# Stick-breaking attention: ordinary transfers issued by GpSimd, transposing ones by SyncE, and four split tiles instead of three

## The chip, the cores and the metric

The kernel runs on one core of a Trainium2 chip. The core has a matrix engine (TensorE, PE; its weight loads are shown as PEld), VectorE (DVE), ScalarE (ACT), GpSimd (POOL) and SyncE (SP), which computes nothing and only issues transfers. Each engine works through its own queue of instructions in order; semaphores join them. 16 DMA engines move the data. The metric is the device time of one execution in microseconds; lower is better.

## The reference

A decoder of two layers over 1024 positions of width 1024, in float32: a recurrent block (RG-LRU), a dense SwiGLU block, then stick-breaking attention with 16 heads of 64, and a second SwiGLU block, with RMS norms before each. The change touches the attention alone:

```python
def stick_breaking_attention(x, w_qkv, w_o):
    qkv = jnp.einsum("bsd,de->bse", x, w_qkv).reshape(bsz, seq, 3, N_HEADS, HEAD_DIM)
    ...
    for blk in range(seq // Q_BLOCK):
        ...
        z = jnp.einsum("bhqd,bhkd->bhqk", qb, kb).astype(jnp.float32) * scale
        ...
        log_fail = jnp.where(strict, jax.nn.log_sigmoid(-z), 0.0)
        suffix = lax.cumsum(log_fail, axis=3, reverse=True) - log_fail
        weights = jnp.where(strict, jnp.exp(jax.nn.log_sigmoid(z) + suffix), 0.0)
        outs.append(jnp.einsum("bhqk,bhkd->bhqd", weights.astype(vb.dtype), vb))
    ...
    return jnp.einsum("bse,ed->bsd", o, w_o)
```

## The kernel before

Matrix products in float32 are made from split operands: a tile is written as a high part and a rest (`hi`, `lo`), and three products are summed (`mm3`). In the attention the operands are half-precision pairs or float32 pairs, made in the same way.

The attention works on pairs of heads, `q` = 0 to 7. For each pair, `qkv_steps` projects queries, keys and values (`which` = 0, 1, 2) in two halves of 512 positions. It is a generator that yields after every `mm3`, so that its matrix products can be set between those of the pair before: it is the "fill". What it yields is handled by `evacuate`:

- Queries and keys are split into `two` and copied by ordinary transfers into the tiles `q` (four transfers per half, 128 KB each) and `kk` (four per half, 256 KB each), because the parts have to change partitions.
- Values are split into `vx` and brought into `v` by two transposing transfers per half.
- The weight columns for the projections come by `load_raw`, 512 KB each, three per pair, into the tiles `raw`; `load_link` asks for the one after the next.

The scores of one chunk of 128 queries by up to 512 keys are made by `z_part` on PE; `z_rest` (ACT, a sigmoid) and `scan` (DVE, a running product) turn them into the tile `w`; `turn_weights` splits that into the half-precision tile `wx`, first part by ACT (L1676), rest by DVE (L1677), and one transposing transfer (L1681) brings `wx` into `wt`. `av_part` (PE, L1699) multiplies `wt` by `v`. There are 24 chunks and 24 such products ("units") per pair; the chunks run 8 units ahead.

When a row of units is done, `gather` collects the output in `oo`, `add_v` adds the values (L1715, on GpSimd, or on VectorE for the last pair), and `parts` scales and splits it (ACT L1722, DVE L1723). Most of these outputs are parked in device memory (`od`), two transfers each, since their tiles `xh`, `xl` still hold the input of the projections; `bring_back` reloads them when the projections of the last pair are done, 12 transfers for the first half and 14 after the second. `xh`, `xl` are named `vh`, `vl` or `xg` in the trace.

These small jobs wait in the list `later`, of which one is done per unit. The order of all instructions is written out by hand: each engine executes in the order in which the program lists them (`manual_schedule`). SyncE issues every transfer of the attention, the ordinary and the transposing ones, in one queue. Each pool's `bufs` says how many copies of a tile there are: three of `wx`, two of `vx`. The program is built with 1024 bytes of storage for transfers that GpSimd issues (`dynamic_dma_scratch_size=1024`); before the change it issues none.

Of the kernel before, what the change touches and what calls it, by code (L numbers as in the profile page):

```python
# [11 lines left out]
F16 = mybir.dt.float16  # L12
# [5 lines left out]
P = 128  # L18
S = 1024
D = 1024  # L20
ND = D // P
# [13 lines left out]
def trunk(  # L35
# [21 lines left out]
    nc = tc.nc  # L57
    f32 = lambda t: t.bitcast(F32)
# [42 lines left out]
    xh, xl = [None] * ND, [None] * ND  # L101
# [8 lines left out]
    cp.tile([P, 136], F32, name="edge_l")  # L110


    def load_raw(src, shape):
        raw = rp.tile([P, D], F32, tag="raw", name="raw")
        view = raw if len(shape) == 1 else raw.rearrange("p (a b) -> p a b", a=shape[0])
        nc.sync.dma_start(view, src)
        return raw

    def split(raw, pool=None, tag="w", bufs=None, lo_eng=None, parts=1):
# [9 lines left out]
    def cols(w, c0, n=P):  # L129
        return w[:, c0 : c0 + n].rearrange("(k p) c -> p k c", p=P)  # L130
# [24 lines left out]
    class Mix:  # L155
# [5 lines left out]
            for i in range(ahead):  # L161
                self.proc(i)

        def load(self, i):
            self.raw[i] = load_raw(cols(self.src, self.order[i] * P), (ND,))

        def proc(self, i):
            raw = self.raw.pop(i)
# [91 lines left out]
    with ExitStack() as st, tc.manual_schedule(engines={E.PE, E.Activation, E.DVE, E.Pool, E.SP}):  # L260
# [20 lines left out]
        for i in range(2):  # L281
            src = w_in[i * NB : (i + 1) * NB, D : D + P].rearrange("(k p) c -> p k c", p=P)
# [112 lines left out]
    with ExitStack() as st:  # L395
# [17 lines left out]
        two = lp.tile([P, ND], I32, name="two")  # L413
# [136 lines left out]
        with tc.manual_schedule(engines={E.PE}):  # L550
            for what in "A0 A1 B0 A2 G0 A3 Y0 B1 Y1 A4 G1 A5 B2 Y2 A6 G2 A7 B3 Y3 B4 Y4 G3 B5 Y5 B6 Y6".split():
                {"A": stage_a, "B": stage_b, "G": stage_g, "Y": stage_y}[what[0]](int(what[1]))
            mix = last_tile(ND - 1)
# [833 lines left out]
    def finish(h, w, R, pp, rows):  # L1387
# [75 lines left out]
    w_qkv, wq0 = attn_w_qkv[0], []  # L1463
# [10 lines left out]
    od = {  # L1474
        (q, n): [dp.tile([P, NB], F32, name=f"od{x}{q}_{n}") for x in "hl"]
        for n in range(NH)
        for q in range(NP)
        if kept(q, n)
    }

    pos, obs, begun = ExitStack(), ExitStack(), {}
    with ExitStack() as st:
        ap = st.enter_context(tc.tile_pool(name="ap", bufs=1))
        qs, mix = ExitStack(), [Mix(w_o, 0)]
# [13 lines left out]
        Q, KK, VV, VT = {}, {}, {}, {}  # L1498
# [5 lines left out]
        later, raws, sv, av_ = [], {}, {}, {}  # L1504

        def bring_back(*which):
            for q, n in which:
                nc.sync.dma_start(f32(xh[q][n]), od[q, n][0])
                nc.sync.dma_start(f32(xl[q][n]), od[q, n][1])


        def load_link(i):
            q, which = divmod(i, 3)
            if q < NP:
                raws[i] = load_raw(cols(w_qkv, which * D + q * P), (ND,))
            else:
                mix[0].load(which)

        def column_norms(raw, q):
            sq = ap.tile([P, ND, P], BF16, tag="sq", name="sq", bufs=1)  # L1520
# [62 lines left out]
        def evacuate(q, which, n, ps):  # L1583
            full = lambda tag, m: [ap.tile([P, m, S], F32R, tag=tag, name=tag, bufs=4 if m == 1 else 3) for _ in range(2)]
            cs = slice(n * NB, (n + 1) * NB)
            if which == 2:
                if n == 0:
                    VT[q] = ap.tile([P, S + 1], F32, tag="vt", name="vt", bufs=2)
                    nc.gpsimd.memset(VT[q][:, 0:1], 0.0)
                    VV[q] = ap.tile([P, 2, NT, 2, HD], F16, tag="v", name="v", bufs=2)  # L1590
                t = ap.tile([P, NB], F32, tag="t", name="t", bufs=2)
                after = VT[q][:, n * NB + 1 : (n + 1) * NB + 1]
                nc.vector.scalar_tensor_tensor(after, ps, f32(sv[q]), rbc[n], op0=ALU.mult, op1=ALU.mult)
                yield
                nc.vector.tensor_sub(t, VT[q][:, cs], after)
                vx = ap.tile([P, 4, 2, P], F16, tag="vx", name="vx", bufs=2)
                t3 = t.rearrange("p (b c) -> p b c", b=4)
                nc.scalar.activation(vx[:, :, 0], t3, AF.Copy, scale=1 / UP)
                nc.vector.scalar_tensor_tensor(vx[:, :, 1], t3, 1 / UP, vx[:, :, 0], op0=ALU.mult, op1=ALU.subtract)
                for hx, a in enumerate((top, bot)):  # L1600
                    nc.sync.dma_start(
                        VV[q][:, hx, 4 * n : 4 * n + 4].rearrange("p b h c -> p (b h) c"),
                        vx[a].rearrange("p b h c -> p (b h c)"),
                        transpose=True,
                    )
                if q == NP - 1 and n == 0:
                    bring_back(*((p, 0) for p in range(NP - 2)))
                return
            two = ap.tile([P, 2, NB], F32R, tag="two", name="two", bufs=2)
            if which == 0:  # L1610
                t = ps
                if n == 0:
                    Q[q] = [x[:, 0] for x in full("q", 1)]
            else:
                t = ap.tile([P, NB], F32, tag="t", name="t", bufs=2)
                nc.vector.tensor_mul(t, ps, rbc[n])
                if n == 0:
                    KK[q] = full("kk", 2)
            nc.scalar.copy(two[:, 0], t)
            if which == 0:  # L1620
                nc.vector.tensor_sub(two[:, 1], t, f32(two)[:, 0])
            yield
            if which == 1:
                nc.vector.tensor_sub(two[:, 1], t, f32(two)[:, 0])
            for hx, (a, b) in enumerate(((top, bot), (bot, top))):
                if which == 0:
                    nc.sync.dma_start(f32(Q[q][hx])[a, cs], f32(two)[a, 0])
                    nc.sync.dma_start(f32(Q[q][hx])[b, cs], f32(two)[a, 1])
                else:
                    for half_ in (top, bot):  # L1630
                        nc.sync.dma_start(f32(KK[q][hx])[half_, :, cs], f32(two)[a])


        W = {}
# [37 lines left out]
        def turn_weights(q, hx, j, ci, c0, c1, diag):  # L1672
            F = W[q, hx, j, ci].rearrange("p (b c) -> p b c", c=P)
            m = F.shape[1]
            wx = ap.tile([P, 4, 2, P], F16, tag="wx", name="wx", bufs=3)
            nc.scalar.copy(wx[:, 0:m, 0], F)  # L1676
            nc.vector.tensor_sub(wx[:, 0:m, 1], F, wx[:, 0:m, 0])  # L1677
            g = (q, hx, j // 4, ci)
            if g not in T:
                T[g] = ap.tile([P, 8, 4, P], F16, tag="wt", name="wt", bufs=3)  # L1680
            nc.sync.dma_start(  # L1681
                T[g][:, 0 : 2 * m, j % 4], wx[:, 0:m].rearrange("p b h c -> p (b h c)"), transpose=True
            )
# [7 lines left out]
        def av_part(q, hx, G, kb, first, last):  # L1691
            q0 = max(kb - 4 * G, 0)
            if first:
                av[0] = psO.tile([P, NB], F32, tag="o", name="av_ps")
            ps = av[0]
            lhsT = VV[q][:, hx, kb]
            for part in range(2):
                rhs = T[q, hx, G, kb // 4][:, 2 * (kb % 4) + part, q0:]
                nc.tensor.matmul(  # L1699
                    ps[:, q0 * P :], lhsT=lhsT, rhs=rhs, start=first and part == 0, stop=last and part == 1  # L1700
                )
            if not last:
                return
            a, b = (top, bot)[:: 1 if hx == 0 else -1]

            def gather():
                if hx == 0:
                    oo[q, G] = ap.tile([P, NB], F32, tag="oo", name="oo", bufs=2)
                o = oo[q, G]
                nc.scalar.copy(o[a], ps[b])  # L1710
                nc.vector.tensor_add(o[a], ps[a], o[a])

            def add_v():
                eng = nc.vector if q == NP - 1 else nc.gpsimd
                eng.tensor_add(oo[q, G], oo[q, G], VT[q][:, G * NB + 1 : (G + 1) * NB + 1])  # L1715

            def parts():
                o = oo[q, G]
                down = f32(av_[q])

                def both(hi, lo):
                    nc.scalar.activation(hi, o, AF.Copy, scale=down)  # L1722
                    nc.vector.scalar_tensor_tensor(lo, o, down, f32(hi), op0=ALU.mult, op1=ALU.subtract)  # L1723

                if not kept(q, G):
                    both(xh[q][G], xl[q][G])
                else:
                    oh = ap.tile([P, NB], F32R, tag="oh", name="oh", bufs=1)
                    both(oh, o.bitcast(F32R))
                    nc.sync.dma_start(od[q, G][0], f32(oh))  # L1730
                    nc.sync.dma_start(od[q, G][1], o)

            later.insert(0, gather)
            if hx == 1:
                later.extend((add_v, parts))
# [33 lines left out]
        def score(some):  # L1769
            ps = [z_part(*a) for a in some]  # L1770
            while turning:
                turn_weights(*turning.pop(0))
            for a in some:
                z_rest(ps.pop(0), *a)
                scan(*a)
                turning.append(a)

        E = mybir.EngineType
        with tc.manual_schedule(engines={E.PE, E.Activation, E.DVE, E.Pool, E.SP}):


            load_link(1)
            first = qkv_steps(0)
            between = {
# [18 lines left out]
            c = 0  # L1803
# [69 lines left out]
```

## Time and profile before

| | |
|---|---|
| three timed runs, us | 2298.23, 2293.41, 2296.41; median 2296.41 |
| profiled execution, us | 2296.88, with a span of 2295.1 |
| busy in the span | PE 94%, DVE 78%, ACT 50%, POOL 5% |
| DMA queues | SP's 476032 packets, 334.39 MB, 51.7% of 16 engines |
| chain that ended last | PE 73%, DVE 11%, DMA 6% (all of it `wt<-wx`), ACT 6% |
| attention | from about 960 to 1575 us |

A row of the timeline gives the start in us, the duration in us, engine, line, operation, what is written and read, and in brackets the idle time of the engine before it and what ended it. "SPq" is SyncE's queue: its rows are the issuing of transfers, not their duration. A row of the waits gives who waited for whom, the total in us, how often, and the longest. A row of the stretches gives the length, then busy time and count of PE, PEld, DVE, ACT and POOL, the granted clock of PE, the DMA engines' busy share and GB/s. A row of a tile's instructions gives the shortest, median and longest in ns; one of the DMA issues ends with the median time from issue to landing in us.

### The profile page before, as it was taken

Reading aid. Unit: us, or ns where it says so; the run is one execution under the profiler, and the core shown is the slowest. Engines: PE = TensorE matmul, PEld = TensorE weight load, DVE = VectorE, ACT = ScalarE, POOL = GpSimd, SP = SyncE. Lnnn points to the kernel's source line nnn. Section 1 sums busy time; section 2 is a strip of 40 time slices with the busy share of each in tenths; the row PEclk is TensorE's granted clock in tenths of the full one; section 3 lists DMA queues with packets and bytes.
Section 4 is the critical chain, followed back from the end, with each engine's and each line's share of the span. In section 5 each row is a group of like instructions: output and inputs, shape, how many; then the busy total and the mean of one; then the engine's idle time right before and its main releaser. Section 6 shows DMA issues by size and latency. Waiting matters only on the chain.

```text
span 2295.1 us, 27839 instructions
## 1 busy us (share of the span) xinstructions
PE 2148.8 (94%) x9838; PEld 1742.7 (76%) x9838; DVE 1795.2 (78%) x2604; ACT 1136.8 (50%) x1838; POOL 121.2 (5%) x102
## 2 busy tenths in 40 slices
PE   8999999999999999987778878749999999999999
PEld 7888888888888888865556556527888888888887
DVE  7888588888887888867677776746788888878886
ACT  6676445444445455645445444434454444444556
POOL 1222010000000000000000000001100000000002
PEclk9999999999999999999898989869999999999999
DMA  6111422344447745477777776786223444477452
GB/s 221 55 38 56 156 74 92 115 134 156 138 155 267 244 139 159 129 148 156 141 168 149 158 151 146 155 206 194 74 87 111 137 153 141 152 255 263 147 154 90
DMA packets 476331, 336.43 MB, mean 147 GB/s; under 512 B 187288, under 2 KB 383008, under 8 KB 476192
## 3 DMA queue, kind: packets, MB, share of 16 engines
q1 hardware_dynamic: 476032, 334.39, 51.7%
q8 instruction: 77, 1.26, 0.2%
q14 instruction: 62, 0.51, 0.1%
q10 hardware_dynamic: 160, 0.27, 0.0%
HBM read 184.09 MB, written 83.36 MB: 117 GB/s over the span
## 4 chain that ended last, share of the span: by engine, by line
PE 73%; DVE 11%; DMA 6%; ACT 6%; issue 3%; SPq 1%; DVEq 0%; ACTq 0%
PE p_ps L143 16%; PE p_ps L145 16%; PE p_ps L144 16%; DMA wt<-wx 6%; DVE w L1665 3%; PE a_ps L144 2%; PE a_ps L145 2%; DVE w L1668 2%; PE a_ps L143 2%; PE ob_ps L143 2%; PE ob_ps L144 2%; PE ob_ps L145 2%; ACT wx L1676 2%; ACT w L1658 2%; DVE wx L1677 2%
## 5 line engine op out<-in xcount | busy, mean ns | idle before, releaser
L1677 DVE TENSOR_TENSOR wx<-w,wx 128x128 f16<-128x128 f32 (+1 forms) x192 | 107.2, 559 | 138.4 <-ACT wx L1676 135.5
L1676 ACT CAST wx<-w 128x128 f16<-128x128 f32 (+1 forms) x192 | 98.0, 510 | 227.5 <-DMA wt<-wx 113.3
L143 PE MATMUL p_ps<-vh,wbh 128*128 128x512 f32 x524 | 204.8, 391 | 0.0
L144 PE MATMUL p_ps<-vl,wbh 128*128 128x512 f32 x524 | 204.5, 390 | 0.0
L145 PE MATMUL p_ps<-vh,wbl 128*128 128x512 f32 x524 | 204.2, 390 | 0.2 <-DVE wbl L722 0.2
L143 PE MATMUL p_ps<-vh,wch 128*128 128x512 f32 x524 | 204.2, 390 | 0.0
L145 PE MATMUL p_ps<-vh,wcl 128*128 128x512 f32 x524 | 204.0, 389 | 0.0
L144 PE MATMUL p_ps<-vl,wch 128*128 128x512 f32 x524 | 203.9, 389 | 0.0
L718 ACT CAST wbh<-sb 128x1024 fp32r<-128x1024 f32 (+2 forms) x69 | 69.6, 1009 | 191.6 <-DVE sb L702 191.6
L1699 PE MATMUL av_ps<-wt,v 128*128 128x512 f16 (+3 forms) x384 | 107.3, 366 | 60.1 <-DMA wt<-wx 51.3
L145 PE MATMUL p_ps<-vh,wal 128*128 128x512 f32 x396 | 154.3, 390 | 0.1
L143 PE MATMUL p_ps<-vh,wah 128*128 128x512 f32 x396 | 154.1, 389 | 0.0
L144 PE MATMUL p_ps<-vl,wah 128*128 128x512 f32 x396 | 154.1, 389 | 0.0
L143 PE MATMUL qk_ps<-vh,whi 128*128 128x512 f32 x264 | 140.3, 532 | 0.0
L1658 ACT ACTIVATE w<-z_ps,rs 128x128 f32<-128x128 f32 (+1 forms) x192 | 110.7, 577 | 21.8 <-PE z_ps L1646 21.4
L1645 PE MATMUL z_ps<-kk,q 128*128 128x256 f32 (+1 forms) x192 | 75.8, 395 | 47.3 <-ACT w L1658 44.7
L1665 DVE TENSOR_TENSOR_SCAN w<-w,unit 128x128 f32<-128x128 f32 (+3 forms) x128 | 112.4, 879 | 6.6 <-ACT w L1658 2.9
L145 PEld LDWEIGHTS p_ps<-vh,wbl 128*128 128x128 f32 x524 | 98.4, 188 | 22.3 <-DVE wbl L722 1.5
L145 PEld LDWEIGHTS p_ps<-vh,wcl 128*128 128x128 f32 x524 | 98.4, 188 | 21.1 <-DVE wcl L732 0.6
L143 PEld LDWEIGHTS p_ps<-vh,wch 128*128 128x128 f32 x524 | 98.4, 188 | 20.5 <-ACT tb L1177 0.2
L144 PEld LDWEIGHTS p_ps<-vl,wch 128*128 128x128 f32 x524 | 98.4, 188 | 20.3
L143 PEld LDWEIGHTS p_ps<-vh,wbh 128*128 128x128 f32 x524 | 98.6, 188 | 19.2 <-ACT ta L1177 0.2
(396 smaller groups left out, 5781.2 us busy)
## 6 DMA issues: line engine op xcount, KB each, us to landing
raw<-in_ffn_w_in SPq DMA_DIRECT2D x88, 512.0 KB, 4.0
vl<-pd SPq DMA_DIRECT2D x128, 256.0 KB, 3.6
pd<-U SPq DMA_DIRECT2D x90, 256.0 KB, 2.3
kk<-two SPq DMA_DIRECT2D x64, 256.0 KB, 4.2
raw<-in_ffn_w_out SPq DMA_DIRECT2D x56, 256.0 KB, 3.6
raw<-in_attn_w_qkv SPq DMA_DIRECT2D x24, 512.0 KB, 4.9
h<-hd SPq DMA_DIRECT2D x32, 256.0 KB, 5.5
hd<-h SPq DMA_DIRECT2D x32, 256.0 KB, 2.0
```

Of the source, the lines that this page charges most:

```text
L143: nc.tensor.matmul(ps, lhsT=wh, rhs=mh, start=first, stop=False, **kw)
L144: nc.tensor.matmul(ps, lhsT=wh, rhs=ml, start=False, stop=False, **kw)
L145: nc.tensor.matmul(ps, lhsT=wl, rhs=mh, start=False, stop=last, **kw)
L718: nc.scalar.copy(self.full(self.wb), self.full(self.sb))
L1645: nc.tensor.matmul(ps[:, 0 : c1 - c0], lhsT=lhsT, rhs=KK[q][hx][:, 0, c0:c1], start=True, stop=False)
L1658: nc.scalar.activation(F, ps[:, 0:n], AF.Sigmoid, scale=rs[:, j : j + 1])
L1665: nc.vector.tensor_tensor_scan(rev, rev, unit[:, NB - n :][:, ::-1], 0.0, op0=ALU.mult, op1=ALU.add)
L1668: nc.vector.tensor_tensor_scan(rev, rev, rev, first, op0=ALU.mult, op1=ALU.bypass)
L1676: nc.scalar.copy(wx[:, 0:m, 0], F)
L1677: nc.vector.tensor_sub(wx[:, 0:m, 1], F, wx[:, 0:m, 0])
L1699: nc.tensor.matmul(ps[:, q0 * P :], lhsT=lhsT, rhs=rhs, start=first and part == 0, stop=last and part == 1)
```

## The change

Ordinary transfers of the attention go from SyncE's queue to GpSimd's: the copies into `q` and `kk`, the parking of outputs and their reloading, and the weight loads that `load_link` asks for. A weight load on GpSimd is issued as two halves of four blocks each. SyncE keeps the transposing transfers of `wx` and `vx`. `wx` has four tiles instead of three; `vx` has one instead of two. No arithmetic and no matrix product is changed, and the other engines' order stays.

```diff
-    def load_raw(src, shape):
+    def load_raw(src, shape, queue=nc.sync):
         raw = rp.tile([P, D], F32, tag="raw", name="raw")
         view = raw if len(shape) == 1 else raw.rearrange("p (a b) -> p a b", a=shape[0])
-        nc.sync.dma_start(view, src)
+        if queue is nc.sync:
+            queue.dma_start(view, src)
+        else:
+            for i in range(2):
+                c = slice(i * D // 2, (i + 1) * D // 2)
+                queue.dma_start(raw[:, c].rearrange("p (k c) -> p k c", c=P), src[:, 4 * i : 4 * i + 4])
         return raw
...
-        def load(self, i):
-            self.raw[i] = load_raw(cols(self.src, self.order[i] * P), (ND,))
+        def load(self, i, **kw):
+            self.raw[i] = load_raw(cols(self.src, self.order[i] * P), (ND,), **kw)
...
         def bring_back(*which):
             for q, n in which:
-                nc.sync.dma_start(f32(xh[q][n]), od[q, n][0])
-                nc.sync.dma_start(f32(xl[q][n]), od[q, n][1])
+                nc.gpsimd.dma_start(f32(xh[q][n]), od[q, n][0])
+                nc.gpsimd.dma_start(f32(xl[q][n]), od[q, n][1])
...
-                raws[i] = load_raw(cols(w_qkv, which * D + q * P), (ND,))
+                raws[i] = load_raw(cols(w_qkv, which * D + q * P), (ND,), queue=nc.gpsimd)
             else:
-                mix[0].load(which)
+                mix[0].load(which, queue=nc.gpsimd)
...
-                vx = ap.tile([P, 4, 2, P], F16, tag="vx", name="vx", bufs=2)
+                vx = ap.tile([P, 4, 2, P], F16, tag="vx", name="vx", bufs=1)
...
-                    nc.sync.dma_start(f32(Q[q][hx])[a, cs], f32(two)[a, 0])
-                    nc.sync.dma_start(f32(Q[q][hx])[b, cs], f32(two)[a, 1])
+                    nc.gpsimd.dma_start(f32(Q[q][hx])[a, cs], f32(two)[a, 0])
+                    nc.gpsimd.dma_start(f32(Q[q][hx])[b, cs], f32(two)[a, 1])
                 else:
                     for half_ in (top, bot):
-                        nc.sync.dma_start(f32(KK[q][hx])[half_, :, cs], f32(two)[a])
+                        nc.gpsimd.dma_start(f32(KK[q][hx])[half_, :, cs], f32(two)[a])
...
-            wx = ap.tile([P, 4, 2, P], F16, tag="wx", name="wx", bufs=3)
+            wx = ap.tile([P, 4, 2, P], F16, tag="wx", name="wx", bufs=4)
...
-                    nc.sync.dma_start(od[q, G][0], f32(oh))
-                    nc.sync.dma_start(od[q, G][1], o)
+                    nc.gpsimd.dma_start(od[q, G][0], f32(oh))
+                    nc.gpsimd.dma_start(od[q, G][1], o)
```

Line numbers in the changed kernel are 5 higher from `split` on. Two places show how the queues differ. First SyncE's queue in the second pair, from its second half of the keys to the parking of an output, before:

```order
L1681 DMA_TRANSPOSE wt_8607<-wx_8663 128x8x128
L1631 DMA kk_8551<-two_8656 64x2x512 x2
L1631 DMA kk_8552<-two_8656 64x2x512 x2
L116 DMA raw_8679<-in_attn_w_qkv 128x8x128
L1681 DMA_TRANSPOSE wt_8607<-wx_8691 128x8x128
L1681 DMA_TRANSPOSE wt_8715<-wx_8712 128x2x128
L1681 DMA_TRANSPOSE wt_8715<-wx_8732 128x4x128
L1730 DMA odh0_0_7883<-oh_8739 128x512
L1731 DMA odl0_0_7884<-oo_8409 128x512
```

After it, SyncE's queue from the same transposing transfer on (the numbers of the tiles differ by a few):

```order
L1686 DMA_TRANSPOSE wt_8613<-wx_8669 128x8x128
L1686 DMA_TRANSPOSE wt_8613<-wx_8698 128x8x128
L1686 DMA_TRANSPOSE wt_8722<-wx_8719 128x2x128
L1686 DMA_TRANSPOSE wt_8722<-wx_8739 128x4x128
L1686 DMA_TRANSPOSE wt_8722<-wx_8767 128x6x128
L1606 DMA_TRANSPOSE v_8761<-vx_8778 128x8x64 x2
L1686 DMA_TRANSPOSE wt_8722<-wx_8793 128x8x128
```

The keys, the load and the parking are gone from between the transposes. They stand in GpSimd's queue, where before, in the same stretch, only these instructions stood (`sv` and `av` are scale factors of a pair, `oo` the addition of the values, the memset a column of `vt`):

```order
L1536 TENSOR_SCALAR sv<-nh 128x1
L1537 TENSOR_SCALAR av<-nh 128x1
L1715 TENSOR_TENSOR oo<-oo,vt 128x512
L1589 MEMSET vt 128x1
L1715 TENSOR_TENSOR oo<-oo,vt 128x512
```

GpSimd's queue in that stretch after the change:

```order
L1636 DMA kk<-two 64x2x512 x4
L1541 TENSOR_SCALAR sv<-nh 128x1
L1542 TENSOR_SCALAR av<-nh 128x1
L1636 DMA kk<-two 64x2x512 x4
L121 DMA raw<-in_attn_w_qkv 128x4x128 x2
L1720 TENSOR_TENSOR oo<-oo,vt 128x512
L1735 DMA odh_0_7883<-oh 128x512
L1736 DMA odl_0_7884<-oo 128x512
L1594 MEMSET vt 128x1
L121 DMA raw<-in_attn_w_qkv 128x4x128 x2
L1720 TENSOR_TENSOR oo<-oo,vt 128x512
```

The first addition `oo` now stands behind the transfers of the keys and the two halves of a load; the second behind two halves of the next load. At the end of the attention, the last addition on GpSimd stands behind all 26 reloads in the same way.

## The prediction

> **What bounds the kernel now.** I read the page first, then the stretches, then who waits for whom inside the attention, and last the timeline of single waits.
>
> ```profile
> span 2295.1 us, 27839 instructions
> ```
>
> The profiled execution took 2296.88 us, 1.8 us around its span; the median of the three timed runs is 2296.41 us, so sums made against 2296.9 us hold for the median within 0.5 us. The stretches show where time can be had.
>
> ```profile
> core 0: us, PE busy (x) PEld busy (x) DVE busy (x) ACT busy (x) POOL busy (x), PEclk, DMA share, GB/s
> 1100.00:1200.00 100.00, 76.61 (x339) 55.71 (x338) 70.40 (x100) 47.45 (x91) 4.83 (x9) 0.90 0.75 156
> 1700.00:2295.00 595.00, 589.38 (x2817) 495.21 (x2815) 490.77 (x753) 289.36 (x470) 13.72 (x10) 1.00 0.49 159
> ```
>
> Outside the attention TensorE (PE) is full (589 of 595 us). Inside it, in 1100 to 1200, no engine is: PE 77, VectorE (DVE) 70, ScalarE (ACT) 47, GpSimd (POOL) 5 of 100 us, and the DMA engines 0.75. So it is bound by waits, and the list of waits for 930 to 1560 us names them.
>
> ```profile
> DVE wx L1677 <- ACT wx L1676: 134.1, 87, 10.9
> ACT wx L1676 <- DMA wt<-wx: 113.3, 34, 11.7
> PE av_ps L1699 <- DMA wt<-wx: 51.3, 17, 5.5
> ```
>
> The second row is the root: ACT writes a split tile `wx`, of which there are three, and 34 times it waits until the transposing transfer of the tile three before has landed; DVE then waits for ACT, and PE for the same landings. Each pair of heads (about 71 us) has one long wait of this kind and two short ones.
>
> The long one, site A (six times), is behind four `kk` transfers and a weight load in SyncE's (SP's) queue:
>
> ```profile
> 1049.97 3.38 SPq L1631 DMA_DIRECT2D kk<-two  x4
> 1051.89 1.19 POOL L1715 TENSOR_TENSOR oo<-oo,vt 128x512 f32<-128x512 f32 x1 [11.07 <-DVE oo L1711]
> 1053.39 1.19 SPq L116 DMA_DIRECT2D raw<-in_attn_w_qkv  x1
> 1054.45 0.71 ACT L1722 ACTIVATE oh<-oo,av 128x512 fp32r<-128x512 f32 x1
> 1054.69 5.85 SPq L1681 DMA_TRANSPOSE wt<-wx  x3
> 1060.68 0.51 ACT L1676 CAST wx<-w 128x384 f16<-128x384 f32 x1 [5.52 <-DMA wt<-wx]
> ```
>
> A short one, site B (seven times), is behind the `q` transfers and another load; the other, site C (seven times), is behind the transposes of the values, which stay on SP:
>
> ```profile
> 1095.87 1.90 SPq L1628 DMA_DIRECT2D q<-two  x1
> 1097.82 0.60 SPq L116 DMA_DIRECT2D raw<-in_attn_w_qkv  x1
> 1098.51 4.12 SPq L1681 DMA_TRANSPOSE wt<-wx  x3
> 1103.46 0.51 ACT L1676 CAST wx<-w 128x384 f16<-128x384 f32 x1 [2.76 <-DMA wt<-wx]
> ...
> 1065.03 2.51 SPq L1601 DMA_TRANSPOSE v<-vx  x2
> 1067.63 3.86 SPq L1681 DMA_TRANSPOSE wt<-wx  x3
> 1070.50 0.51 ACT L1676 CAST wx<-w 128x384 f16<-128x384 f32 x1 [2.20 <-DMA wt<-wx]
> ```
>
> Near the end stand three longer waits, once each: X behind `kk` and two loads, Y behind twelve reloads of parked outputs, Z behind fourteen more.
>
> ```profile
> 1483.56 3.38 SPq L1631 DMA_DIRECT2D kk<-two  x4
> 1496.03 0.51 ACT L1676 CAST wx<-w 128x384 f16<-128x384 f32 x1 [7.91 <-DMA wt<-wx]
> ...
> 1505.37 0.51 SPq L1508 DMA_DIRECT2D vh<-odh  x1
> ...
> 1513.21 3.81 SPq L1681 DMA_TRANSPOSE wt<-wx  x3
> 1518.29 0.62 ACT L1676 CAST wx<-w 128x512 f16<-128x512 f32 x1 [11.72 <-DMA wt<-wx]
> ...
> 1527.97 2.51 SPq L1601 DMA_TRANSPOSE v<-vx  x2
> 1530.53 0.57 SPq L1508 DMA_DIRECT2D vh<-odh  x1
> 1533.03 0.71 ACT L1722 ACTIVATE vh<-oo,av 128x512 fp32r<-128x512 f32 x1
> ...
> 1530.55 1.59 POOL L1715 TENSOR_TENSOR oo<-oo,vt 128x512 f32<-128x512 f32 x1 [43.86 <-DVE oo L1711]
> ...
> 1545.00 0.40 ACT L1676 CAST wx<-w 128x256 f16<-128x256 f32 x1 [11.26 <-DMA wt<-wx]
> ```
>
> **The change part by part.** It takes from SP's queue everything but the transposes, puts it on GpSimd's, and gives ACT a fourth `wx`. What a transfer costs GpSimd no row shows: before, it issues none. The bounds are these rows and GpSimd's own longest work in the attention, the 1.59 us addition above:
>
> ```profile
> L1627 SPq DMA_DIRECT2D q<-two x32: 551/594/1210, 966.6 to 1457.4; - x32
> L1631 SPq DMA_DIRECT2D kk<-two x64: 591/663/1374, 978.5 to 1485.6; - x64
> q<-two SPq DMA_DIRECT2D x64, 128.0 KB, 2.4
> raw<-in_attn_w_qkv SPq DMA_DIRECT2D x24, 512.0 KB, 4.9
> ```
>
> From 0.6 us (SP's issue) to 1.6 us; nothing lies near one end, so I take the middle, 1.1 us. A load is now two halves. Between them GpSimd may have to wait: at least nothing, at most one landing, 4.9 us for the whole load; I take 2.4 us, the quickest landing in these rows, which is also half of 4.9.
>
> The first and the last of ACT's seven waits at B, then of the seven at C:
>
> ```profile
> 1032.43 0.51 ACT L1676 CAST wx<-w 128x384 f16<-128x384 f32 x1 [2.10 <-DMA wt<-wx]
> ...
> 1466.02 0.51 ACT L1676 CAST wx<-w 128x384 f16<-128x384 f32 x1 [3.00 <-DMA wt<-wx]
> ...
> 1012.10 0.62 ACT L1676 CAST wx<-w 128x512 f16<-128x512 f32 x1 [2.19 <-DMA wt<-wx]
> ...
> 1431.09 0.51 ACT L1676 CAST wx<-w 128x384 f16<-128x384 f32 x1 [3.16 <-DMA wt<-wx]
> ```
>
> *Site B.* `q` and the load are off SP's queue, and a fourth `wx` lets ACT run one chunk further. The wait goes: halfway between its first and last 2.6 us, 7 x 2.6 = 18 us. What is late next is PE itself.
>
> *Site C.* The transposes of `v` remain ahead; only the fourth tile helps. ACT's wait, 2.7 us by the same reckoning, goes; but PE waits for landings half as often as ACT (17 times against 34), so I count half: 7 x 1.3 = 9 us. Bounds: 0 and 19 us.
>
> *Site A.* The wait for the transposes goes, and another comes in its place. GpSimd's queue now holds, in this order, four `kk`, two halves of a load, and only then the addition L1715, whose result ACT reads at L1722. In order of time: 4 x 1.1 + 2 x 1.1 + 2.4 between the halves + 1.2 for the addition = 10.2 us after 1049.97, so 1060.2. ACT was at L1722 at 1054.45. It stands 5.7 us where it stood 5.5 us, and behind it in ACT's order stand the next sigmoid and split, for which DVE and PE wait. Six times: a gain of 0 (-1). Bounds: at 0.6 us and no wait between halves 4.8 us, 0.3 us of standing, +5.2 us each; at 1.6 us and 4.9 us 15.7 us, -5.7 us each.
>
> *Site X.* The same with two loads: 8 x 1.1 + three waits of 2.4 + 1.2 = 17.2 us after `kk`. ACT needs the sum 4.5 us after `kk`, as at A: 12.7 us of standing against 7.9: -5 us. Bounds +6 and -16 us.
>
> *Site Y.* SP spent 7.8 us (1505.37 to 1513.21) on twelve reloads before the transposes. These now start earlier, but share the DMA engines with the 3 MB of the reloads. Between 0 and 7.8 us: +4.
>
> *Site Z.* Fourteen reloads on GpSimd from about 1528 (when SP could not yet issue them for the `v` transposes): 15.4 us, then the addition, 1.6 us, for the last output: 1545.0. ACT reads it at L1722, at 1533.03 before: it stands 12 us against 11.3: -1 us. Bounds +6 and -8 us.
>
> *Start.* The first score waits for four `kk`: 4 x 0.44 us more: -2 us (0 to -8).
>
> *`vx` from two to one.* ACT writes the next `vx` about 10 us after the one before it, and the transposes of `v` have landed long before: nothing. If their landing took over 10 us it would cost the difference.
>
> The Trainium skill, DMA: Bandwidth & Descriptors, in its sections Terms and SWDGE vs HWDGE vs iDMA, says that GpSimd writes each descriptor, 16 bytes, into rings kept in SBUF. The kernel sets 1024 bytes aside; an estimate from that page is 64 entries an engine, into which two halves of 33 do not fit, so that the wait between halves would be a whole landing and the sum some 20 us worse, about no change. No run here shows it yet.
>
> Sum: 18 + 9 - 1 - 5 + 4 - 1 - 2 = 22 us off 2296.9, that is 2275 us.
>
> **The rivals.**
>
> *GpSimd is as quick as SP.* For it: it has nothing else to do (4.8 of 100 us). Against it: its two additions shown take 1.2 and 1.6 us. At 0.6 us and no wait between halves, A gives 31, X 6, Y 8, Z 6, B 18, C 19: 88 us, 2209 us. Chance 0.13.
>
> *GpSimd's queue becomes the bound (slower).* The place is A: the addition L1715 behind `kk` and the load. Each 0.1 us more per transfer costs 0.6 us at each A (3.6 us), 0.8 at X, 1.4 at Z and about 0.6 at the start: 6.4 us. The 22 us are used up at 1.1 + 0.34 = 1.45 us per transfer; from there it is slower. At 1.6 us, with 4.9 us between halves: -34 at A, -16 at X, -8 at Z, -8 at the start, 0 at Y, +27 at B and C: 39 us slower, 2336 us. For it: GpSimd runs in order, and ACT reads what stands last. Chance 0.25.
>
> *The transposes wait for the same bytes.* The DMA share is 0.75, so the four `kk` and the load may hold up the transposes from whichever queue they come. Then B, C and Y bring nothing, and A, X, Z and the start cost what they cost: 9 us slower, 2306 us. Against it: SP issues without a break from 1049.97 to 1060.54 at A, and there the order of issue delays too. Chance 0.13. The Trainium skill, DMA: Bandwidth & Descriptors, section Issuing engines are not separate DMA queues, says this outright: all queues run on the same 16 engines, and another issuer saves only its sequencer's time. By that rule the time is this rival's.
>
> *Nothing comes of it:* PE and DVE are themselves late where ACT waited, and gains and losses cancel: 2297 us. Chance 0.05.
>
> **How the numbers follow.** The forecast, 2275 us, has a chance of 0.44. A measurement of this kernel can tell about 0.2% (5 us) from no change. Faster by more than that: nearly all of the forecast (0.42) and the first rival (0.13), 0.55. Within it: 0.08. Slower: 0.25 and most of 0.13, 0.37. The range, 2235 to 2320 us, takes in the forecast with issue costs from 0.8 to 1.4 us, the third and fourth rival, and the nearer half of the first and second; what lies beyond on either side has about 0.1 each. The forecast's own range is 2255 to 2295 us.
>
> **What would show it.** Right: in the waits of the attention "ACT wx <- DMA wt<-wx" falls from 113 us to under 40; the wait of ACT at L1722 (by then L1727) for the addition on GpSimd, absent now, stands at 4 to 7 us at each A; GpSimd's transfers take about 1.1 us each, with a gap of some 2 us between the halves of a load. Wrong: transfers of 0.7 us or below, or of 1.5 us or above; a wait for `wt` that stays near 113 us; a wait of PE's scores for `kk` or `q`; DVE's operations longer beside GpSimd's issues than before.

## The result and the profile after

The changed kernel takes 2298.12 us, the median of 18 runs (2289.98 to 2306.24). The kernel before, run beside it, takes 2296.64 us, also of 18. The ratio is 1.0007, with a 95% interval of 0.9998 to 1.0017: no change that can be told. The forecast was 2275 us. The profiled execution has a span of 2291.9 us against 2295.1 us before.

First a stretch in the middle of the attention, in the columns shown for before:

```profile
1100.00:1200.00 100.00, 78.39 (x358) 56.16 (x356) 68.16 (x100) 46.61 (x90) 26.24 (x44) 0.95 0.81 159
```

In these 100 us the trace has 358 matrix products of PE instead of 339, at a granted clock of 0.95 instead of 0.90; GpSimd went from 5 to 26 us, and no engine is full: the attention is still bound by waits. The middle did become faster. ACT's rows at the sixth site A, of before and then of after:

```profile
1420.30 0.51 ACT L1676 CAST wx<-w 128x384 f16<-128x384 f32 x1 [5.90 <-DMA wt<-wx]
...
1412.69 0.72 ACT L1727 ACTIVATE oh<-oo,av 128x512 fp32r<-128x512 f32 x1 [9.51 <-POOL oo L1720]
```

The first site A is at 1060.68 before and at 1061.62 after (below), so that a pair of heads took 71.9 us before and takes 70.2 now, 8.5 us less in five pairs. The start and the end of the attention gave this back, all but the 3.2 us by which the span fell. The list of waits from 930 to 1575 us shows that they are other ones (lines are 5 higher than before):

```profile
POOL raw L121 <- issue: 109.8, 30, 6.5
ACT oh L1727 <- POOL oo L1720: 72.2, 7, 14.3
ACT wx L1681 <- DMA wt<-wx: 32.0, 7, 11.9
PE av_ps L1704 <- DMA wt<-wx: 8.8, 8, 1.6
PE z_ps L1650 <- DMA kk<-two: 7.3, 5, 2.3
```

The wait for `wt` did what the prediction asked of it: ACT's fell from 113.3 us to 32.0, PE's from 51.3 to 8.8. PE's scores wait for `kk` a little (7.3 us, 0.6 before). But ACT now stands 72.2 us for GpSimd's addition, seven times. One of the seven is 14.3 us (site X), so the six at site A have (72.2 - 14.3) / 6 = 9.65 us each, where ACT stood 5.5 to 5.9 us for `wt` before. The first of the six in the timelines of GpSimd and of ACT:

```profile
1048.97 2.43 POOL L1636 DMA_DIRECT2D kk<-two  x4 [9.69 <-ACT w L1663]
1052.78 0.78 POOL L121 DMA_DIRECT2D raw<-in_attn_w_qkv  x1 [1.38 <-issue]
1059.72 0.75 POOL L121 DMA_DIRECT2D raw<-in_attn_w_qkv  x1 [6.16 <-issue]
1060.49 1.10 POOL L1720 TENSOR_TENSOR oo<-oo,vt 128x512 f32<-128x512 f32 x1
...
1061.62 0.72 ACT L1727 ACTIVATE oh<-oo,av 128x512 fp32r<-128x512 f32 x1 [9.51 <-POOL oo L1720]
```

In GpSimd's rows the bracket is time in which it did nothing that the profile shows. 6.16 us lie between the two halves of one load (5.81 to 6.55 us at the six sites A), and 1.38 us ahead of the first; both are put down to "issue", that is, to no semaphore. The first row of the list adds them up, 30 waits of this kind and 109.8 us. The landings of the two halves at this place (shortest, median, longest):

```profile
DMA to landing us min/median/max: 3.4/5.0/6.6
```

The longer, 6.6 us, is the first half's: issued at 1052.78, it landed at 1059.4, and the second was issued at 1059.72. The issuing itself is short, by GpSimd's groups (last number before the second bar: mean ns of one):

```profile
L1636 POOL DMA_DIRECT2D kk<-two x64 | 38.6, 609 | 90.1 <-ACT w L1663 62.9 <-ACT wx L1681 23.2 <-DVE two L1629 4.0
L1632 POOL DMA_DIRECT2D q<-two x32 | 16.9, 527 | 43.9 <-ACT two L1624 43.5
```

At the end of the attention ACT waits for `wt` at Y and Z as before, and SyncE's queue, which holds transposes and hardly anything else now, is slow. Three rows of ACT and one of SyncE, from the timeline:

```profile
1514.44 0.62 ACT L1681 CAST wx<-w 128x512 f16<-128x512 f32 x1 [11.87 <-DMA wt<-wx]
1520.53 0.62 ACT L1681 CAST wx<-w 128x512 f16<-128x512 f32 x1 [4.88 <-DMA wt<-wx]
1536.91 0.62 ACT L1681 CAST wx<-w 128x512 f16<-128x512 f32 x1 [10.90 <-DMA wt<-wx]
...
1510.29 26.27 SPq L1686 DMA_TRANSPOSE wt<-wx  x3
```

Three transposing transfers stretch over 26.27 us of SyncE's queue, what waits lie between them included, where three took 3.81 us at Y before. The transposes' own rows, of before and then of after, are durations of issuing in ns (shortest, median, longest), and from issue to landing in us:

```profile
L1681 SPq DMA_TRANSPOSE wt<-wx x192: 1167/1235/3642, 988.6 to 1568.9; - x192
DMA to landing us min/median/max: 2.3/2.8/6.3
```

```profile
L1686 SPq DMA_TRANSPOSE wt<-wx x192: 1167/1258/14673, 986.3 to 1564.2; - x192
DMA to landing us min/median/max: 2.3/4.0/17.7
```

### The profile page after: what moved, and what is told of

It is laid out like the page before. It is cut to its first block, busy times and chain, and to the rows that moved or that the text cites. A ratio compares the mean times of both kernels' runs of the same rounds, so it can differ in the third digit from the quotient of the medians.

```text
span 2291.9 us, 28023 instructions
## 1 busy us (share of the span) xinstructions
PE 2137.0 (93%) x9838; PEld 1728.4 (75%) x9838; DVE 1787.2 (78%) x2604; ACT 1135.0 (50%) x1838; POOL 261.1 (11%) x334
## 4 chain that ended last, share of the span: by engine, by line
PE 73%; DVE 10%; issue 7%; ACT 5%; DMA 4%; POOL 2%; DVEq 0%; ACTq 0%
PE p_ps L150 16%; PE p_ps L148 16%; PE p_ps L149 16%; DMA wt<-wx 4%; DVE w L1670 3%; DVE w L1673 3%; PE a_ps L149 2%; PE a_ps L150 2%; PE a_ps L148 2%; PE ob_ps L149 2%; PE ob_ps L148 2%; PE ob_ps L150 2%; ACT wx L1681 2%; ACT w L1663 2%; DVE wx L1682 1%
## 5 line engine op out<-in xcount | busy, mean ns | idle before, releaser
L1650 PEld LDWEIGHTS z_ps<-kk,q 128*128 128x128 f32 x192 | 38.9, 202 | 133.4 <-ACT w L1663 117.4
L148 PE MATMUL qk_ps<-vh,whi 128*128 128x512 f32 x264 | 133.5, 506 | 0.0
L223 POOL TENSOR_TENSOR acc<-acc,rbc 128x512 f32<-128x512 f32 x30 | 40.7, 1357 | 772.5 <-ACT rbc L222 772.5
L121 POOL DMA_DIRECT2D raw<-in_attn_w_qkv x46 | 35.5, 771 | 752.3 <-DVE g L1186 623.2
```

Source lines behind the costliest of these rows:

```text
L148: nc.tensor.matmul(ps, lhsT=wh, rhs=mh, start=first, stop=False, **kw)
L223: (eng or nc.gpsimd).tensor_add(acc[n], acc[n], sq)
L1650: nc.tensor.matmul(ps[:, 0 : c1 - c0], lhsT=lhsT, rhs=KK[q][hx][:, 0, c0:c1], start=True, stop=False)
```

## The experiments

Each time is the median of four executions. The kernel before, run beside them in three sets, took 2295.46, 2295.86 and 2297.47 us; the ratios are to it. Two theories stood against each other from the start. **Storage:** the second half of a load waits for room for its descriptors, with the addition behind it, and this standing eats the gain. **Starving:** the transposes on SyncE get too little of the DMA engines while GpSimd's queue has work.

**Twice the storage for GpSimd's descriptors (e1).** The changed kernel with

```diff
-dynamic_dma_scratch_size=1024
+dynamic_dma_scratch_size=2048
```

> The changed kernel with 2048 bytes instead of 1024 set aside for GpSimd's transfers. Theory 1 (the wait between the halves): in the changed kernel GpSimd waits 5.8 to 6.4 us between the two halves of the load at each site A, since both do not fit into its storage; ACT then stands 9.3 to 10.1 us at L1727. With room for both, the addition follows after 2.4 + 1.5 + 1.1 us, ACT stands 1 to 2 us, and about 8 us come back at each of six sites A and 10 at X: 2298 falls to 2230 to 2255 us. Theory 2 (the transposes wait for the same bytes): the load's data then comes all at once, the transposes land as much later, and ACT's wait for wt, 32 us in the changed kernel, rises by 40 us or more: 2285 to 2300 us.

2257.01 us, ratio 0.9845 (0.9816 to 0.9874). The same place on GpSimd, and two rows of the waits:

```profile
1048.33 2.44 POOL L1636 DMA_DIRECT2D kk<-two  x4 [10.04 <-ACT w L1663]
1050.76 1.53 POOL L121 DMA_DIRECT2D raw<-in_attn_w_qkv  x2
1052.31 1.80 POOL L1720 TENSOR_TENSOR oo<-oo,vt 128x512 f32<-128x512 f32 x1
```

```profile
ACT wx L1681 <- DMA wt<-wx: 65.5, 21, 13.0
ACT oh L1727 <- POOL oo L1720: 23.8, 7, 8.9
```

Both halves now follow the `kk` at once, and ACT's wait for the addition fell from 72.2 to 23.8 us. One number in the kernel was worth some 37 us (a ratio of 1.0007 against 0.9845). So the wait between the halves is for room in that storage: this theory is shown, though the time lies 2 us above its range. Room can still run out: at X, where four halves follow each other, the fourth waits 7.33 us, and ACT the 8.9 us of the second row. The wait for `wt` doubled, by 33.5 us where the second theory asked for 40 or more, so that theory is not excluded. The trace is of an execution of 2269.49 us, 12 us above the median, so its waits need not be those of the median.

**The addition on VectorE (e2).** The storage stays at 1024; nothing that ACT reads stands behind the halves any more.

```diff
-                eng = nc.vector if q == NP - 1 else nc.gpsimd
+                eng = nc.vector
```

> The changed kernel with the addition of the values (L1720) on VectorE for every pair, so that ACT waits for nothing on GpSimd. Theory 1: the standing at A (9.6 us six times) and X (14.3 us) goes, 14 additions of about 0.7 us come to VectorE, 10 us: 2298 falls to 2240 to 2260 us. Theory 2: the transposes of that time are late anyway, ACT stands for wt instead: 2285 to 2300 us.

2270.82 us, 0.9891 (0.9865 to 0.9918), above the 2240 to 2260 us of the first theory and below the second's range. It brought some 70% of what the storage brought (1.16 of 1.62% against the changed kernel). Part of what is left shows in the waits:

```profile
DVE t L1600 <- POOL vt L1594: 51.8, 8, 10.9
```

DVE now waits for a clearing of one column of `vt`, 0.12 us of work that stands on GpSimd behind the same halves. This wait was there in the changed kernel once, at the start (4.83 us). Not the addition costs, but any step of GpSimd that another engine waits for.

**The move without the tiles (e3).** The changed kernel with `wx` at 3 tiles and `vx` at 2.

> The changed kernel with three tiles of wx and two of vx as before: the move of the transfers alone. If the fourth tile is what removed ACT's wait for wt (113 to 32 us), that wait comes back to 60 us or more and the time is 2310 to 2330 us; if the move did it, the wait stays near 32 us and the time at 2295 to 2302 us.

2341.3 us, 1.0192 (1.0167 to 1.0217), above the 2310 to 2330 us expected if the fourth tile is what removed the wait for `wt`. That wait came back:

```profile
ACT wx L1681 <- DMA wt<-wx: 72.0, 26, 10.3
ACT oh L1727 <- POOL oo L1720: 70.3, 7, 12.5
```

Though `q` and the loads are off SyncE's queue, ACT still waits about 2 us at each B and about 3 us at each C. At A the wait for `wt` is gone, and the wait for the addition stands in its place.

**The tiles without the move (e4).** The kernel before with

```diff
-                vx = ap.tile([P, 4, 2, P], F16, tag="vx", name="vx", bufs=2)
+                vx = ap.tile([P, 4, 2, P], F16, tag="vx", name="vx", bufs=1)
...
-            wx = ap.tile([P, 4, 2, P], F16, tag="wx", name="wx", bufs=3)
+            wx = ap.tile([P, 4, 2, P], F16, tag="wx", name="wx", bufs=4)
```

> The kernel before with four tiles of wx and one of vx: the tiles alone, all transfers on SyncE. If ACT's waits come from the number of tiles, each shrinks by about one chunk (3 us): 6 x 3 at A, 18 at B, 9 at C, 9 at the end, 2296.5 falls to about 2245 us. If PE's own wait for the landings (51 us) takes over, since a landing is not earlier than before, 2280 to 2297 us.

2250.37 us, 0.9803 (0.9787 to 0.9819). Together the two say where the change went: the tiles alone take 45 us off (1.97%), the move alone adds 44 us (1.92%), and both at once give nothing. Counted from site A to site A as above, a pair takes 65.7 us with the tiles alone and 77.0 us with the move alone. In the list of waits of the tiles alone, and in ACT's timeline at the first A:

```profile
PE av_ps L1699 <- DMA wt<-wx: 56.6, 20, 5.5
ACT wx L1676 <- DMA wt<-wx: 35.7, 12, 10.3
...
1051.02 0.71 ACT L1722 ACTIVATE oh<-oo,av 128x512 fp32r<-128x512 f32 x1
1052.14 0.51 ACT L1676 CAST wx<-w 128x384 f16<-128x384 f32 x1 [0.41 <-DVE w L1665]
```

SyncE still issues four `kk` and a load ahead of these transposes, and ACT does not stand: the fourth tile covers site A by itself, 5.5 us and all. The reason to move the queues was gone once there were four tiles. PE's wait for `wt` stayed (51.3 before, 56.6 now) while 45 us went, so these did not come from it.

**What is left of the move.** Twice the storage still leaves 2257 us against 2250. Four kernels part it by what is on which queue. First the weight loads back on SyncE, whole (e5):

```diff
-                raws[i] = load_raw(cols(w_qkv, which * D + q * P), (ND,), queue=nc.gpsimd)
+                raws[i] = load_raw(cols(w_qkv, which * D + q * P), (ND,))
...
-                mix[0].load(which, queue=nc.gpsimd)
+                mix[0].load(which)
```

> The changed kernel with the weight loads (whole, not halved) back on SyncE's queue; q, kk, parked outputs and reloads stay on GpSimd. Theory 1 (the addition that ACT reads stands behind two halves whose second waits for ring space): GpSimd's queue at A is four kk and the addition, so ACT's standing at A falls from 9.6 to under 2.5 us, as with twice the storage (2257 us): 2250 to 2262 us. Theory 2 (GpSimd's wide packets hold the transposes up): the loads' share of that goes as well, ACT's wait for wt lies below the 65.5 us of the run with twice the storage. Rival (SyncE's queue is where it hurts, so a load ahead of the transposes costs): waits of 2 to 3 us for wt come back at B and C, 2275 us or more.

2268.83 us, 0.9867 (0.9819 to 0.9914): above the 2250 to 2262 us of the first theory, below the rival's 2275.

```profile
ACT wx L1681 <- DMA wt<-wx: 72.7, 22, 14.5
PE z_ps L1650 <- DMA kk<-two: 29.8, 7, 5.9
```

ACT's standing at A is gone, as expected (0.5 us each), with the storage still at 1024: GpSimd's queue has no load there to make room for. But PE's scores now wait for `kk`, once in each pair: the load runs beside it instead of behind it. The transfers of `kk` from 930 to 1575 us, of before and then of e5, with the median time to landing at the end:

```profile
kk<-two SPq DMA_DIRECT2D x64, 256.0 KB, 4.2
```

```profile
kk<-two POOLq DMA_DIRECT2D x64, 256.0 KB, 7.7
```

In the changed kernel, where the load stands behind `kk` in GpSimd's queue, it was 5.2 us.

The wait for `wt`, 72.7 us, did not fall below the 65.5 us of e1 as the second theory wanted.

Then loads and reloads both on SyncE, so that of this traffic only `q`, `kk` and the parking stay on GpSimd (e9):

> The changed kernel with the weight loads (whole) and the reloads back on SyncE's queue; only q, kk and the parked outputs stay on GpSimd, storage 1024 bytes. Tiles alone took 2250 us, the loads alone taken back 2269 us. If q and kk on GpSimd's queue cost by themselves (kk lands late beside a load that runs at the same time, 7.7 us against 4.2 us, and PE's scores wait for it 3 to 6 us in each pair): 2258 to 2266 us, and PE's wait for kk stays near 29.8 us. If the reloads on GpSimd were what was left: 2248 to 2254 us, and PE's wait for kk makes no difference.

2256.67 us, 0.9831 (0.9812 to 0.985). It lies between the ranges of the two readings, 1.3 us under the first, and the row on which the first rests is there: `kk` costs PE as much as in e5.

```profile
PE z_ps L1650 <- DMA kk<-two: 30.3, 7, 5.5
```

So the reloads on GpSimd cost about 12 us in e5 against e9, and `q` and `kk` on GpSimd about the 6 us that remain to the tiles alone; in both comparisons the intervals still overlap, so these two are sizes and not verdicts.

Twice the storage, with the reloads on SyncE (e6) and on ScalarE (e7):

```diff
-                nc.gpsimd.dma_start(f32(xh[q][n]), od[q, n][0])
+                nc.sync.dma_start(f32(xh[q][n]), od[q, n][0])      # e6; nc.scalar in e7; the same for xl
```

> The changed kernel with 2048 bytes of descriptor storage, and with the 52 reloads of parked outputs back on SyncE's queue. Against the run with the storage alone (2257 us; waits of ACT for wt near the end 13.0, 6.2 and 7.9 us, slowest landing of a transposing transfer 17.7 us). Theory 2 (transposes starve beside GpSimd's reloads): the slowest landing falls under 8 us, the waits near the end to about 24 us in all as with tiles alone: 2250 to 2256 us. Rival (what counts is that the bytes move, not from which queue): landings as before, 2257 us within 3.

> The changed kernel with 2048 bytes of descriptor storage, and with the 52 reloads issued by ScalarE, whose queue uses packets of 2048 bytes where GpSimd's uses 4096. It costs ScalarE about 26 x 0.5 = 13 us of issuing near the end, most of it where it stands anyway. If the width of the packets starves the transposes: slowest landing about half of 17.7 us, 9 us. If any second queue does it: 15 us or more. If only GpSimd's queue does it for a reason of its own: under 7 us. Time 2250 to 2265 us in each case, so the landings decide and not the time.

2253.94 us, 0.9813 (0.9789 to 0.9838), and 2262.71 us, 0.9847 (0.9829 to 0.9865). And twice the storage, all reloads on GpSimd, with rows of 2048 bytes that do not touch each other in DRAM (e10):

```diff
-        (q, n): [dp.tile([P, NB], F32, name=f"od{x}{q}_{n}") for x in "hl"]
+        (q, n): [dp.tile([P, NB + 128], F32, name=f"od{x}{q}_{n}")[:, 0:NB] for x in "hl"]
```

> The changed kernel with 2048 bytes of descriptor storage, and with the rows of the parked outputs in DRAM 640 numbers apart instead of 512, so that a row of 2048 bytes no longer touches the next. All reloads stay on GpSimd. With the storage alone: transposing transfers from 1440 to 1530 us land after a median of 6.2 us, at most 17.7; with the reloads on ScalarE's queue 2.8 and 10.3. If the 4096-byte records of GpSimd's queue are two neighbouring rows and their width is what starves the transposes: records of 2048 bytes for the reloads, and landings near the second pair of numbers. If it is GpSimd's queue as such: landings near the first, whatever the records' size.

2261.53 us, 0.9848 (0.983 to 0.9866). The landings of the transposes of `wx` from 1440 to 1530 us, in the order e1 (reloads on GpSimd), e6 (SyncE), e7 (ScalarE), e10 (GpSimd, padded):

```profile
DMA to landing us min/median/max: 2.4/6.2/17.7
```

```profile
DMA to landing us min/median/max: 2.3/2.9/11.8
```

```profile
DMA to landing us min/median/max: 2.3/2.8/10.3
```

```profile
DMA to landing us min/median/max: 2.4/4.7/19.1
```

In e6 the slowest landing was to fall under 8 us; it is 11.8. And the 2.8 us of e7 do not say that these transposes ran undisturbed beside ScalarE's reloads. ACT writes `wx`, and while it stands at the reloads it writes none. The first and the last of the first twelve reloads in e7 ("ACTq" is ScalarE's queue), and SyncE's queue at that time:

```profile
1463.13 0.36 ACTq L1513 DMA_DIRECT2D vh<-odh  x1
...
1475.09 0.44 ACTq L1514 DMA_DIRECT2D xg<-odl  x1
...
1464.51 2.58 SPq L1606 DMA_TRANSPOSE v<-vx  x2
1476.26 5.01 SPq L1686 DMA_TRANSPOSE wt<-wx  x3
```

Only the transposes of `v` were issued among the reloads, here and again among the fourteen later ones. The landings of `v`, of the one pair in e1 that was issued beside GpSimd's reloads, and then of the two pairs in e7:

```profile
DMA to landing us min/median/max: 15.7/15.7/15.7
```

```profile
DMA to landing us min/median/max: 7.5/8.6/9.8
```

In e10 one pair issued among GpSimd's reloads took 17.9 us; before the change `v` landed after a median of 2.7 us. So the transposes are late beside either queue, about twice as late beside GpSimd's as beside ScalarE's; these are four pairs of transfers, so a size and not a law. Queues of e1, e7 and e10 from 1440 to 1530 us (packets, MB, share of the 16 engines; q0 is GpSimd's, q10 ScalarE's, q1 SyncE's):

```profile
q0 software_dynamic: 3200, 10.49, 50.4%
q1 hardware_dynamic: 22796, 5.87, 44.9%
```

```profile
q10 hardware_dynamic: 3744, 6.82, 27.9%
```

```profile
q0 software_dynamic: 2880, 9.44, 43.9%
```

SyncE's queue in e1 moves packets of some 260 bytes on average. GpSimd's moves 10.49 MB in 3200 packets, in 26 reloads and 14 other transfers; ScalarE's moves its 26 reloads, 6.82 MB, in 3744. Without 16 tiny packets that report completion for each transfer, the packets of data come to 4096 and 2048 bytes: twice the width, and about twice the landing, as the expectation of e7 had it for the width (9 us). But the padding did not make GpSimd's packets smaller (9.44 MB in 2880, again 4096 bytes; `wx` landed after a median of 4.7 and up to 19.1 us). Nor do rows that touch in DRAM make them wide: the halves of the loads, with rows of 512 bytes, move in packets of the same size (1.05 MB in 324 packets from 1052 to 1060 us in the changed kernel). So e10 could not tell the packets' width from another property of GpSimd's queue: that stays open. The Trainium skill, DMA: Bandwidth & Descriptors, section Queues, rings and completion order, says that each DMA engine takes turns between queues a whole packet at a time; narrow packets beside wide ones would then lose, which these rows agree with and do not prove. In time e7 gained nothing over e1: ACT itself stood at its two rows of reloads, 11.81 and 13.96 us.

**What helps beyond the tiles.** With four tiles and everything on SyncE, the next weight load is asked for three steps later in the list of things to do (e8):

```diff
-                for i in (at + 1,) if at < 3 * NP else (at + 1, at + 2):
-                    load_link(i)
+                ask = lambda at=at: [load_link(i) for i in ((at + 1,) if at < 3 * NP else (at + 1, at + 2))]
+                if q == 0 and which == 0:
+                    ask()
+                else:
+                    later.insert(3, ask)
```

> The kernel before with four split tiles and one vx, all transfers on SyncE (2250 us with the load where it was), and the weight load of the next link asked for three steps later in the list of things to do, away from the four kk. If queue order on SyncE still matters with four tiles: the remaining waits of PE for wt (56.6 us, 20 times) shrink and the time falls by 2 to 10 us. If the fourth tile covers all of it: within 3 us of 2250. If the load comes too late for the projection that needs it: slower.

2242.34 us, 0.976 (0.9741 to 0.9779), 8 us under the tiles alone. Then the reloads no longer in two long rows but one output (e11) or two (e12) at each step of the loop over units:

```diff
-                    bring_back(*((p, 0) for p in range(NP - 2)))
+                    back.extend((p, 0) for p in range(NP - 2))
...
+                for _ in range(1):          # e12: range(2)
+                    if back:
+                        bring_back(back.pop(0))
```

> The kernel before with four split tiles, the later weight load (2242 us), and the reloads of parked outputs no longer in two rows of 12 and 14 on SyncE but two transfers (one output) at each step of the attention. If the transposes near the end wait for what stands ahead of them on SyncE: ACT's two waits of 12.2 and 10.1 us fall under 4 us each, and up to 18 us go: 2225 to 2236 us. If they wait for bytes, the same bytes move in the same time: 2238 to 2246 us. If the reloads come too late for the output projection, PE waits for vh: slower than 2242 us.

> The same with four transfers (two outputs) at each step: the reloads done sooner, the transposes behind four at a time. Between the run with all at once (2242 us) and the run with two at a step; if the output projection waits for the reloads there, this one is the fastest.

2231.42 us, 0.9719 (0.9702 to 0.9737), and 2235.41 us, 0.9738 (0.9722 to 0.9754); the two cannot be told apart. The end of the attention in e8 and in e11:

```profile
ACT wx L1679 <- DMA wt<-wx: 31.0, 10, 12.2
PE av_ps L1702 <- DMA wt<-wx: 19.6, 13, 2.8
...
1430.00:1510.00 80.00, 52.10 (x201) 32.75 (x200) 47.18 (x63) 31.02 (x61) 6.76 (x6) 0.79 0.81 198
```

```profile
ACT wx L1679 <- DMA wt<-wx: 11.6, 7, 4.9
...
1430.00:1510.00 80.00, 61.69 (x229) 37.85 (x228) 51.33 (x70) 33.26 (x64) 6.75 (x5) 0.83 1.01 231
```

In e8 PE's wait for `wt` had fallen to 19.6 us (56.6 with the tiles alone). In e11 ACT's longest wait for `wt` is 4.9 us instead of 12.2, not quite under the 4 expected. PE works 62 of these 80 us instead of 52, and the DMA engines' share rises from 0.81 to 1.01, which is to be read as full: not the bytes were in the way at Y and Z, but the order in which SyncE issued them. e11 is the fastest kernel of the study, 2.8% under the kernel before, with nothing on GpSimd's queue.

## Why the prediction was wrong

The mechanism at A was named in the prediction and is what happened; the step that failed is its size, the 2.4 us taken for GpSimd's waiting at the two halves of a load. At the first A it was 7.5 us, and with room for the descriptors (e1), which takes this waiting away at A, the kernel is some 37 us faster.

| term | forecast, us | in the trace after, us |
|---|---|---|
| Site A | -1 | six standings, 9.65 instead of 5.8: -23 |
| Site B | +18 | ACT's waits gone: +18 |
| Site C | +9 | gone too, all of it: +19 |
| Site X | -5 | 14.3 instead of 7.9: -6 |
| Site Y | +4 | 11.9 + 4.9 instead of 11.7: -5 |
| Site Z | -1 | 10.9 instead of 11.3: 0 |
| Start | -2 | ACT 6.5 instead of 1.6: -5 |
| sum | +22 | -2 |

The right column is made of ACT's standings in the two traces and ends at -2 us; the span fell by 3.2 us and the median rose by 1.5, so the account closes within the spread of the runs.

- **Site A.** After the start of `kk` the prediction had 4.4 for four transfers, 2.2 for two halves, 2.4 between them and 1.2 for the addition, 10.2 us. The trace has 2.4, then 1.4 of waiting, 0.8, 6.2 of waiting, 0.8 and 1.1: 12.6 us. The transfers were quicker than taken (0.53 to 0.78 us, near SyncE's 0.6) and the waiting three times longer (7.5 us). ACT came to its place at 3.1 us instead of 4.5, since the fourth tile had freed it, so it stood 9.5 us and not 5.7. The bounds, nothing to 4.9 us, did not hold it: 4.9 was the landing of a whole load on SyncE's queue, and here half of one took 6.6 us.
- **The estimate was there.** What the prediction worked out from the Trainium skill, DMA: Bandwidth & Descriptors (sections Terms and SWDGE vs HWDGE vs iDMA), and left out of its sum, was 64 entries, two halves that do not fit, a whole landing of waiting, and about no change. The trace agrees (5.8 to 6.6 us between the halves at A), and e1 shows that the storage sets this wait; how many entries it holds no run shows.
- **Sites B and C.** The size at B held, but only one of its two reasons: with the move alone (e3) ACT still waits about 2 us there, so it was the fourth tile that took the wait away and not the clearing of SyncE's queue. At C half was counted because PE waits for landings half as often as ACT. e4 shows that reasoning wrong: PE's waits for `wt` stayed while the time went.
- **Credit for A.** The prediction weighed the fourth tile at B and C and let the move pay for A. e4 shows that the tile pays for A as well, and that the move then has nothing left to win. No step asked what the tiles do with the queues as they are; asked, it would have shown that two halves of the change stand against each other.
- **Sites Y and Z.** Taking the reloads from SyncE did not bring the transposes forward, as they starved beside GpSimd's queue (26.27 us for three). Z was to be set by the addition at the end of GpSimd's queue; it was set by `wt`, and the addition was ready 5 us earlier.
- **Start.** It was to be `kk`; it was the clearing of `vt` behind a load's halves, 4.83 us. PE's scores did wait for `kk` later, five times and 7.3 us in all, which the prediction had named as a sign of being wrong.
- **`vx` from two to one** cost nothing that shows in the changed kernel; with the later load (e8) ACT waits for its landing three times, 7.6 us in all.
- **The rivals.** That GpSimd is as quick as SyncE was right in its premise and useless for the time, since the storage set it. That GpSimd's queue becomes the bound was right in place and mechanism, not by the price of a transfer but by the wait for room; it stopped at no change because B and C gave more than counted. That the transposes wait for the same bytes was wrong at B and C; at Y and Z they did land late beside GpSimd's reloads, and in e7, less so, beside ScalarE's.
- **Two sums of the prediction.** At the start 0.1 us more per transfer costs 4 x 0.1 = 0.4 us, not 0.6, and the bound at 1.6 us is -4, not -8, so the slower rival's 39 us should have been 35. The outcome does not hang on this.

## What to carry to other kernels

When a change gives a waiting engine another buffer and also moves the queue that it waits for, cost each half with the other left out: here the buffer alone hid the wait, and the move had only its price left. Before steps are put on GpSimd's queue, look what stands behind them there that another engine reads, even 0.12 us of it, and whether the descriptors of what is issued in one go fit its storage. A row of transfers that all wait to be issued ahead of something urgent on the same queue was here better spread over the steps than moved to another queue.

## What the hardware showed that was not expected

- GpSimd issued an ordinary transfer in 0.53 to 0.61 us and a half load in 0.77 us, about as quickly as SyncE (0.59 to 0.66 us), as long as there was room; without room it stood 5.8 to 6.6 us at each A, with everything behind it, and no semaphore names the cause.
- Transposing transfers of `v` landed after 15.7 us beside GpSimd's reloads (e1) and after 7.5 and 9.8 us beside ScalarE's (e7), against a median of 2.7 us before; in the changed kernel one transposing transfer took 14.67 us to issue.
- Two queues undid an order that one queue had kept: with the load on SyncE and `kk` on GpSimd, `kk` landed after a median of 7.7 us instead of 4.2, and PE's scores waited for it in every pair.
